# One weight ring and one set of PSUM banks through a hybrid gMLP and forgetting-attention block

## The chip, the cores and the metric

The kernel runs on one core of a Trainium2 chip. The metric is device time in microseconds (us) of one execution. In float32 the whole block is computed to almost full precision: every matmul operand is split into a high part (a cast to `float32r`) and a low part (what the cast lost), and each product is three matmuls, low by high, high by low, high by high.

## The reference

```python
h = rmsnorm(x, norm_mix_g)                       # x: 512 rows x 1024
z = h @ w_in                                     # u, v (gMLP), q, k, v (attention), f, two gates
uv = gelu(z[..., :2048]);  z_u, z_v = uv[..., :1024], uv[..., 1024:]
gates = sigmoid(z[..., o3:])                     # 2 x 1024 columns
a = z_u * (W_s @ layernorm(z_v) + b_s)           # per block of 128 rows and group of 128 columns
b = forgetting_attention(q, k, v, f_logit, b_f)  # 16 heads of 64
merged = gate_a * (a @ w_branch_a) + gate_b * (b @ w_branch_b)
x = x + merged @ w_out
h2 = rmsnorm(x); up = causal_depthwise_conv(h2 @ w_up)
x = x + (gelu(up[..., :2816]) * up[..., 2816:]) @ w_down
x = x + (p @ w_ple) * sigmoid(rmsnorm(x) @ w_ple_gate)
return rmsnorm(x)
```

## The kernel before

TensorE (PE) follows an order written out by hand almost everywhere (`tc.manual_schedule(engines={PE})`); ScalarE (ACT), VectorE (DVE), GpSimd (POOL) and the DMA queue of SyncE (SP) each get an order that a planner lays down before the run. At run time each of these queues is worked in that order: what waits holds up what stands behind it.

The stages, in the order of PE's work:

1. **Start.** Rows of `x` come in four blocks of 128. For each block `rms_x` squares and scales it, and `transpose_split` transposes it on PE in two groups of four and splits it into `hT`. A third copy of the transposed rows (`keep`, into the tile `zv`) serves the next stage but one. Between the blocks PE works on the first half of `p @ w_ple` (`pp`) and of the attention's v columns (`pv`). Then the 16 forget logits (`L550`), the second half of v, and gate chunk 0.
2. **Wino.** The u and v columns of gMLP (`wino_jobs`) are products by a 2x2 Strassen-Winograd scheme, seven block products P1, P7, P6, P2, P5, P4, P3 for `zv` and seven for `zu`, each 24 matmuls. Eight raw weight tiles are loaded per set; DVE combines them (`combine`: t3 makes the operand of P7 from tiles (1,1) and (0,1), then t2, t1, t4), `split_w` splits them. Then layernorm of `zv`, whose gains and offsets are broadcast loads into `gb`.
3. **Mix.** Eight `mix(g)` steps (masked block mixing, times u, transposed to DRAM `aT_d`), woven with gate chunks.
4. **Attention.** Eight pairs of heads. While pair `pr` is transposed and multiplied with v, the softmax of pair `pr+1` runs and the q and k projections of pair `pr+2` (`qk_pair`, two chunks of 24 matmuls) and gate chunks (24 matmuls each) fill PE in between (`weave`: items of the attention with `n` fill steps spread over them).
5. **Merge and the rest.** The attention output `o32` is split into `oT`, the last gate chunk runs, then `w_branch_b`, `w_branch_a`, `w_out`, the convolutional FFN and the final stage.

A *gate chunk* is one 128-column piece of the 16 gate projections: a weight load of 512 KB, its split, 24 matmuls, a copy out of PSUM (`place()` gives the SBUF tile) and a store to DRAM. Chunks have no hurry before the merge, so they serve as filler: before the change chunk 0 runs before the wino stage, 1 to 3 in the mix, 4 at the head of attention, one in each of pairs 0 to 5, two in pair 6, two in pair 7, and chunk 15 after attention.

Weights go through a *ring*: `load_w` takes a raw tile, a high and a low tile, issues the load on SP, and casts on ACT (L130) and subtracts on DVE or POOL (L131). There are two rings, one after the other: `ring0` with 8 raw tiles and 4 pairs of split tiles until the mix, and `ring` with 3 raw tiles and 5 pairs from attention on. Small tiles of 4 KB per partition called `mid`, three in all, serve for the forget gate's work (`fm`), gate chunks' copies, `gb`, and the mixing weights `wst`. The eight PSUM banks are shared out three times: four tags of two banks, then `c` 6 and `f` 2 for wino and mix, then `mm` 2, `sc` 2, `pt` 3, `av` 1 for attention, then four tags of two again.

Of the kernel before, what the change touches and what calls it, by code (L numbers as in the profile page):

```python
# [41 lines left out]
def hybrid_block(  # L42
# [24 lines left out]
    small = ctx.enter_context(tc.tile_pool(name="small", bufs=4, side="left"))  # L67
    state = {"n": 0, "bank": 0, "ring": None, "pool": {}, "psum": None}

# [14 lines left out]
    def bank(tag=None):  # L84
        pool, bufs = state["psum"]
        if tag is None:
            tag = f"b{state['bank'] % len(bufs)}"
            state["bank"] += 1
        return pool.tile([P, 512], F32, tag=tag, name=uid("bank"), bufs=bufs[tag])
# [24 lines left out]
    def open_ring(name, nbuf, raw=RAW_BUFS):  # L114
        es, pool = open_pool(name, "left")
        state["ring"] = (pool, nbuf, raw)
        return es


    def load_w(src, a, b, sub=None, later=None):  # L120


        pool, nbuf, nraw = state["ring"]
        raw = pool.tile([P, a, b], F32, tag="raw", name=uid("raw"), bufs=nraw)
        hi = pool.tile([P, a, b], F32R, tag="whi", name=uid("whi"), bufs=nbuf)
        lo = pool.tile([P, a, b], F32R, tag="wlo", name=uid("wlo"), bufs=nbuf)
        nc.sync.dma_start(raw, src)

        def split():
            A.copy(hi, raw)  # L130
            (sub or V).tensor_tensor(lo, raw, hi.bitcast(F32), ALU.subtract)  # L131
        if later is not None:
            later.append(split)
        else:
            split()
        return hi, lo
# [95 lines left out]
    def split_w(raw):  # L232
# [5 lines left out]
        return hi, lo  # L238

    def wino_jobs(wv, c0, act, sums, evac):  # L240


        pool, _, nraw = state["ring"]
        B, banks = {}, {}

        def load():
            for i, h in ((0, 0), (1, 1), (0, 1), (1, 0)):
                B[i, h] = []
                for j in range(2):
                    raw = pool.tile([P, 2, 512], F32, tag="raw", name=uid("raw"), bufs=nraw)  # L250
                    k, c = 4 * i + 2 * j, c0 + 512 * h
                    nc.sync.dma_start(raw, wv[:, k:k + 2, c:c + 512])
                    B[i, h].append(raw)
# [17 lines left out]
        def product(name, a, k0, col, acc, fresh):  # L271

            skip = not fresh

            def f(ws):
                if fresh:
                    banks[acc] = [bank("c") for _ in range(2)]
                for j in range(2):
                    for r in range(2):
                        out_ap, cs = banks[acc][r], ds(col + r * P, P)  # L280
                        for kk in range(2):
                            k = k0 + 2 * j + kk
                            wh, wl = ws[j][0][:, kk, :], ws[j][1][:, kk, :]
                            T.matmul(out_ap, a[1][:, k, cs], wh,  # L284
                                     start=(fresh and j == 0 and kk == 0), stop=False,
                                     skip_group_check=skip)
                            yield
                            T.matmul(out_ap, a[0][:, k, cs], wl, start=False, stop=False,  # L288
                                     skip_group_check=skip)
                            yield  # L290
                            T.matmul(out_ap, a[0][:, k, cs], wh, start=False,  # L291
                                     stop=(j == 1 and kk == 1), skip_group_check=skip)
# [88 lines left out]
    def transpose_split(src, dst, rb, n=NK, keep=None):  # L381

        done = []
        for k0 in range(0, n, 4):
# [7 lines left out]
            done.append((at, bk))  # L392
        if keep is not None:
            for at, bk in done:
                A.copy(keep[at], bk)

    def rms_x(src, g_bc, dst, rb):
# [49 lines left out]
    def zv_tile():  # L447
        return ph.tile([P, 4096], F32, tag="zv", name=uid("zv"))

    def mid(dt=F32):  # L450
        return ph.tile([P, D], dt, tag="mid", name=uid("mid"), bufs=3)

# [10 lines left out]
    with tc.manual_schedule(engines={ET.PE, ET.Activation, ET.DVE, ET.SP}):  # L463
# [36 lines left out]

        warm = mid()[:, 0:P]
        V.memset(warm, 0.0)
# [15 lines left out]
        steps(pp, 6)  # L518
        tx[0]()
        tx.append(rms_x(xt[1], gmix, hT, 1))  # L520
# [3 lines left out]
        steps(pv, 12)  # L524
        tx[1]()
        steps(pv, 12)
    with tc.manual_schedule(engines={mybir.EngineType.PE}):
        for rb in range(2, NB):
            tx.append(rms_x(xt[rb], gmix, hT, rb))
            steps(pv, 8)  # L530
            tx[rb]()
            steps(pv, 16)
        steps(pv, 24)


    fm = [mid(), mid(), mid(F32R)]
    bft = consts.tile([P, 1], F32, tag="bft", name="bft")
# [57 lines left out]

    psum.close()


    psum = open_psum("psumS", WINO_BANKS)
    zv = zv_tile().rearrange("p (b c) -> p b c", b=NB)  # L600
# [14 lines left out]

    def gate_steps(n, tag, place):

        w = load_w(w_in_v[:, :, gate_col(n):gate_col(n) + P], 8, P, sub=None)
        bk = bank(tag)
# [29 lines left out]
    with tc.manual_schedule(engines={ET.PE}):  # L649
        run(gate_steps(0, "f", lambda: mid()[:, 0:512]))  # L650
        units = wino_steps(wino_jobs(w_in_v, 1024, hT, sums, wino_rows(zv, gelu_zv))
                           + wino_jobs(w_in_v, 0, hT, sums, wino_rows(zu, gelu_zu)))
        steps(units, 168)
        gb = [mid(), mid()]
        nc.sync.dma_start(gb[0], rows_bc(ln_g[0], D))
        nc.sync.dma_start(gb[1], rows_bc(ln_b[0], D))

        wst = mid().rearrange("p (g s) -> p g s", g=8)
        nc.sync.dma_start(wst, w_s[0].rearrange("g t s -> t g s"))
# [10 lines left out]
        for rb in range(NB):  # L670
            A.activation(zv[:, rb, :], zv[:, rb, :], AF.Identity, bias=nm[:, rb:rb + 1])
            for h in range(2):
                A.activation(bank("f"), zv[:, rb, 512 * h:512 * h + 512], AF.Square,
                             accum_out=sq[:, NB * h + rb:NB * h + rb + 1])
# [9 lines left out]
        wsT = [quarter(f"S1{t}").rearrange("p (g t) -> p g t", g=8) for t in "hl"]  # L684
        bk = bank("f")
        T.transpose(bk[:, 0:P], bsr, ident)
        V.tensor_copy(bsT, bk[:, 0:NK])
        steps(units, 12)
        for g0 in (0, 4):
            bk = bank("f")  # L690
            for g in range(4):
# [5 lines left out]
        def mix(g):  # L697
# [3 lines left out]
            split_out((vh, vl), zv[:, :, c], (slice(None),) * 3)  # L701
            bk = bank("c")
            mm3(bk, wsT[0][:, g, :], wsT[1][:, g, :], vh, vl, True, True)
# [3 lines left out]
            yield  # L707
            bk = bank("c")
            for n in range(NB):
# [7 lines left out]
        run(units)  # L717

        w_qk0 = qk_weights(0)
        ms = [mix(g) for g in range(NK)]  # L720
# [3 lines left out]
        items += [ms[NK - 2], ms[NK - 1]]  # L724
        fill = chain(*(gate_steps(n, "f", lambda: mid()[:, 0:512]) for n in range(N_FIRST, N_FIRST + N_MIX)))
        weave(items, fill, 24 * N_MIX)
# [3 lines left out]
    ph_es.close()  # L730
    psum.close()
    ring.close()


    ring = open_ring("ring", 5)
    psum = open_psum("psumB", ATT_BANKS)
    att_es, att = open_pool("att", "right")
    o32 = k_view(slot(4, F32))

    for t in ("pth", "ptl"):  # L740
        att.tile([P, 1280], F32R, tag=t, name=uid(t), bufs=2)

# [107 lines left out]
    pts = [[[], []] for _ in range(NPAIR)]  # L850

    with tc.manual_schedule(engines={mybir.EngineType.PE}):
        run(qk_pair(0, w_qk0, qk[0]))
        cm[0], cm[1] = cum_pair(0), None
        sm = [softmax_head(qk[0], cm[0], a, probs[0][a]) for a in range(2)]
        fill = chain(qk_pair(1, qk_weights(1), qk[1]), gate_early(N_FIRST + N_MIX))
        for _ in range(12):
# [3 lines left out]
        for pr in range(NPAIR):  # L861
            fill = [gate_early(n) for n in range(GATES[pr], GATES[pr + 1])]
            n_fill = 24 * len(fill)
            if pr + 2 < NPAIR:
                fill.insert(0, qk_pair(pr + 2, qk_weights(pr + 2), qk[pr + 2]))
                n_fill += 48
# [16 lines left out]
    att_es.close()  # L883
    psum.close()
    psum = open_psum("psumC", FREE_BANKS)

# [13 lines left out]
    with tc.manual_schedule(engines={ET.PE}):  # L900
        for n in range(GATES[-1], N_GATES):
            run(gate_steps(n, None, lambda: scr.tile([P, S], F32, tag="gy", name=uid("gt"), bufs=2)))
    for k0 in (0, 4):
# [22 lines left out]

    def gated(wv, act, n0):

        c0 = P * (n0 % NK)
        sgs = []  # L930
        for i in range(2):
# [3 lines left out]
            sgs.append(sg)  # L935
        py = pieces_T(wv, c0)
        for i in range(2):
# [6 lines left out]
    for c0 in range(0, D, 256):  # L944
        for by, sg, c in gated(w_b_v, oT, c0 // P):
            V.tensor_tensor(sg, by, sg, ALU.mult)
# [254 lines left out]
```

## Time and profile before

| | before |
|---|---|
| median of 3 runs | 985.09 us (984.2 to 985.59) |
| the profiled execution | 985.49 us |
| its span in the profile | 983.7 us |
| PE busy | 943.7 us, 96% |
| DVE, ACT, POOL busy | 594.6, 466.5, 115.2 us |
| HBM traffic | 122 GB/s over the span |
| chain of work that ended last | PE 88%, DVE 6%, ACT 2%, DMA 2%, issue 1%, POOL 1% |

The span is what the profile shows from the first to the last instruction; 1.8 us of the execution lie around it. A time in a timeline row is the start in us from the span's start; the second number is the duration; a bracket at the end says how long the engine had stood idle before the row and what released it. Matmul rows carry modelled ends, so the distance between the starts of two neighbours is the true pace of PE.

### The profile page before, as it was taken

What the parts mean: (1) busy time and instruction counts of PE and PEld (TensorE: products, weight loads), DVE (VectorE), ACT (ScalarE), POOL (GpSimd) and SP (SyncE); (2) the same over time, 40 slices, a digit from 0 to 9 for tenths busy, and PEclk for the clock granted to TensorE, in tenths of its full rate; (3) what the DMA queues carried; (4) which work ended last, traced back from release to release, by engine and by line L of the source; (5) the groups of instructions that cost most, each with busy time, mean ns of one, the idle gap of its engine ahead of it and who ended that gap; (6) DMA issues with size and microseconds to landing.
All of it is one profiled execution on the core that took longest, in us unless ns stands there. A gap on an engine that the chain in (4) does not pass through costs nothing.

```text
span 983.7 us, 11724 instructions
## 1 busy us (share of the span) xinstructions
PE 943.7 (96%) x4375; PEld 780.0 (79%) x4375; DVE 594.6 (60%) x1017; ACT 466.5 (47%) x779; POOL 115.2 (12%) x94
## 2 busy tenths in 40 slices
PE   6999996979999999799999999999999999999996
PEld 5788885867888888688888788888888888888885
DVE  4787888538777788623344756555346663355664
ACT  6554684346666666522334544444124442144453
POOL 2100000022222200000121400000000000000225
PEclk9999998989999999999999999999999999999998
DMA  9352340664333332296864233323223333223202
GB/s 331 128 152 83 121 108 1 220 169 133 106 101 97 97 97 86 65 338 230 265 188 158 65 118 118 106 86 107 90 67 101 110 105 106 86 86 110 75 31 85
DMA packets 102148, 121.21 MB, mean 123 GB/s; under 512 B 5252, under 2 KB 70972, under 8 KB 102092
## 3 DMA queue, kind: packets, MB, share of 16 engines
q1 hardware_dynamic: 101948, 120.21, 38.7%
q8 instruction: 34, 0.56, 0.2%
q10 hardware_dynamic: 144, 0.26, 0.1%
q14 instruction: 22, 0.18, 0.1%
HBM read 106.79 MB, written 13.66 MB: 122 GB/s over the span
## 4 chain that ended last, share of the span: by engine, by line
PE 88%; DVE 6%; ACT 2%; DMA 2%; issue 1%; POOL 1%; SPq 0%; POOLq 0%; DVEq 0%
PE bank L153 17%; PE bank L157 16%; PE bank L155 16%; PE bank L140 5%; PE bank L141 5%; PE bank L139 5%; PE bank L213 3%; PE bank L217 3%; PE bank L215 3%; PE bank L288 2%; PE bank L284 2%; PE bank L291 2%; PE bank L832 2%; PE bank L823 2%; DMA raw<-in_w_in_dram 2%
## 5 line engine op out<-in xcount | busy, mean ns | idle before, releaser
L153 PE MATMUL bank<-slot,wlo 128*128 128x512 f32 (+1 forms) x744 | 297.4, 401 | 11.3 <-DVE wlo L131 6.2
L155 PE MATMUL bank<-slot,whi 128*128 128x512 f32 (+1 forms) x744 | 290.5, 391 | 0.0
L157 PE MATMUL bank<-slot,whi 128*128 128x512 f32 (+1 forms) x744 | 290.4, 391 | 0.0
L130 ACT CAST whi<-raw 128x1024 fp32r<-128x1024 f32 x140 | 145.9, 1047 | 130.7 <-PE bank L141 76.2
L131 DVE TENSOR_TENSOR wlo<-raw,whi 128x1024 fp32r<-128x1024 f32 x116 | 143.1, 1237 | 106.1 <-ACT whi L130 105.5
L153 PEld LDWEIGHTS bank<-slot,wlo 128*128 128x128 f32 x744 | 141.2, 190 | 35.6 <-issue 6.6
L157 PEld LDWEIGHTS bank<-slot,whi 128*128 128x128 f32 x744 | 140.7, 189 | 29.0
L155 PEld LDWEIGHTS bank<-slot,whi 128*128 128x128 f32 x744 | 141.2, 190 | 22.7
L131 POOL TENSOR_TENSOR wlo<-raw,whi 128x1024 fp32r<-128x1024 f32 x24 | 59.4, 2481 | 486.6 <-ACT whi L130 480.9
L139 PE MATMUL bank<-whi,slot 128*128 128x512 f32 (+1 forms) x232 | 88.6, 382 | 0.0
L141 PE MATMUL bank<-whi,slot 128*128 128x512 f32 (+1 forms) x232 | 88.6, 382 | 0.0
L140 PE MATMUL bank<-wlo,slot 128*128 128x512 f32 (+1 forms) x232 | 88.6, 382 | 0.0
L213 PE MATMUL bank<-whi,slot 128*128 128x512 f32 x152 | 60.6, 399 | 2.1 <-DVE slot L352 2.1
L217 PE MATMUL bank<-whi,slot 128*128 128x512 f32 x152 | 60.1, 395 | 0.0
L215 PE MATMUL bank<-wlo,slot 128*128 128x512 f32 x152 | 59.6, 393 | 0.0
L140 PEld LDWEIGHTS bank<-wlo,slot 128*128 128x128 f32 x232 | 43.6, 188 | 8.5
L141 PEld LDWEIGHTS bank<-whi,slot 128*128 128x128 f32 x232 | 43.6, 188 | 8.5
L139 PEld LDWEIGHTS bank<-whi,slot 128*128 128x128 f32 x232 | 43.6, 188 | 8.4
L1041 DVE SCALAR_TENSOR_TENSOR ul<-bank,cvT,ul 128x511 f32<-128x511 f32 x22 | 16.5, 750 | 51.7 <-ACT ul L1040 51.7
L237 DVE TENSOR_TENSOR wlo<-raw,whi 128x1024 fp32r<-128x1024 f32 x28 | 33.9, 1221 | 13.1 <-ACT whi L236 13.0
L805 ACT ACTIVATE t<-t,mn 128x512 f32<-128x512 f32 (+1 forms) x64 | 36.0, 562 | 12.4 <-DVE mn L802 8.9
L236 ACT CAST whi<-raw 128x1024 fp32r<-128x1024 f32 x28 | 29.4, 1051 | 22.8 <-PE bank L291 17.0
(265 smaller groups left out, 1320.5 us busy)
## 6 DMA issues: line engine op xcount, KB each, us to landing
raw<-in_w_in_dram SPq DMA_DIRECT2D x56, 512.0 KB, 4.0
raw<-in_w_up_dram SPq DMA_DIRECT2D x44, 512.0 KB, 3.6
raw<-in_w_down_dram SPq DMA_DIRECT2D x22, 512.0 KB, 3.4
cum<-cum_d SPq DMA_DIRECT2D x8, 512.0 KB, 4.0
raw<-in_w_branch_b_dram SPq DMA_DIRECT2D x8, 512.0 KB, 4.1
slot<-aT_d SPq DMA_DIRECT2D x4, 1024.0 KB, 13.3
sg<-gate_d SPq DMA_DIRECT2D x16, 256.0 KB, 3.8
raw<-in_w_branch_a_dram SPq DMA_DIRECT2D x8, 512.0 KB, 8.7
```

The source lines that it names most:

```text
L130: A.copy(hi, raw)
L131: (sub or V).tensor_tensor(lo, raw, hi.bitcast(F32), ALU.subtract)
L139: T.matmul(out_ap, alo, bhi, start=start, stop=False)
L140: T.matmul(out_ap, ahi, blo, start=False, stop=False)
L141: T.matmul(out_ap, ahi, bhi, start=False, stop=stop)
L153: T.matmul(out_ap, wl, ah, start=(n == 0 and k == 0), stop=False)
L155: T.matmul(out_ap, wh, al, start=False, stop=False)
L157: T.matmul(out_ap, wh, ah, start=False, stop=end)
L213: T.matmul(bk, alo[:, k, r], wh, start=(k == 0), stop=False)
L215: T.matmul(bk, ahi[:, k, r], wl, start=False, stop=False)
L217: T.matmul(bk, ahi[:, k, r], wh, start=False, stop=(k == nk - 1))
L805: A.activation(t, t, AF.Exp, scale=-1.0, bias=m, accum_out=rs[:, i:i + 1])
```

## The change

- One ring (5 split pairs, 3 raw tiles) and one set of banks (`mm` 2, `sc` 2, `pt` 3, `av` 1) live through the whole kernel. Where no tag is named, banks are taken in the order of `BANK_TURN`.
- Until attention begins, a pool `more` of 5 tiles adds to the raw tiles: of every 8 loads, counted through, numbers 1, 2 and 8 go to the ring's own raw tiles and numbers 3 to 7 to `more`. The pool `mid` is gone: gate chunks' copies, `gb` and `wst` take tiles of `more`, and the forget gate's work and the warm-up tile take `S4h`, `S4l` and `S2l`, which the start and the wino sums use too.
- The `keep` copies of a block of rows are issued after the next block's transposes.
- Gate chunk 1 runs alone between wino and mix (`N_COVER`); the mix is woven with chunks 2 to 4, attention begins with 5, and each of pairs 0 to 5 has the chunk one higher; pair 6 has one chunk (12) where it had two.
- During the last chunk of the mix the q and k weights of pairs 0 and 1 are queued; during the last chunk of attention the weights of chunk 15 and of the first 256 columns of `w_branch_b`.

```diff
-GATES = [5, 6, 7, 8, 9, 10, 11, 13, 15]
+GATES = [6, 7, 8, 9, 10, 11, 12, 13, 15]
-FREE_BANKS = {"b0": 2, "b1": 2, "b2": 2, "b3": 2}
-WINO_BANKS = {"c": 6, "f": 2}
-ATT_BANKS = {"mm": 2, "sc": 2, "pt": 3, "av": 1}
+N_COVER = 1
+X_BUFS = 5
+BANKS = {"mm": 2, "sc": 2, "pt": 3, "av": 1}
+BANK_TURN = ["mm", "sc", "pt", "mm", "sc", "pt", "pt", "av"]
...
+    def raw_tile(a, b):
+        pool, _, nraw = state["ring"]
+        if state["more"]:
+            state["raw"] += 1
+            if state["raw"] % (nraw + X_BUFS) >= nraw:
+                return more_tile().rearrange("p (a b) -> p a b", a=a)
+        return pool.tile([P, a, b], F32, tag="raw", name=uid("raw"), bufs=nraw)
+
+    def more_tile():
+        return state["more"].tile([P, D], F32, tag="more", name=uid("more"), bufs=X_BUFS)
...
-        if keep is not None:
+        def copy():
             for at, bk in done:
                 A.copy(keep[at], bk)
+        return copy
...
-    ring = open_ring("ring0", 4, 8)
-    psum = open_psum("psumA", FREE_BANKS)
+    ring = open_ring("ring", 5)
+    more_es, state["more"] = open_pool("more", "left")
+    psum = open_psum("psum", BANKS)
...
-    fm = [mid(), mid(), mid(F32R)]
+    fm = [quarter("S4h", F32), quarter("S4l", F32), quarter("S2l")]
...
-        run(gate_steps(0, "f", lambda: mid()[:, 0:512]))
+        run(gate_steps(0, "mm", lambda: more_tile()[:, 0:512]))
...
         run(units)
-        w_qk0 = qk_weights(0)
+        for n in range(N_FIRST, N_FIRST + N_COVER):
+            run(gate_steps(n, "mm", lambda: more_tile()[:, 0:512]))
...
+        def preload(g):
+            next(g)
+            yield
+            w_qk.extend(qk_weights(pr) for pr in range(2))
+            yield from g
...
+    def preload_merge(g):
+        next(g)
+        yield
+        w_merge.append(gate_weights(N_GATES - 1))
+        w_merge.append(pieces_T(w_b_v, 0))
+        yield from g
```

More of the change, by code (lines that the diff above doesn't have):

```diff
@@ L67, in hybrid_block @@
     small = ctx.enter_context(tc.tile_pool(name="small", bufs=4, side="left"))
-    state = {"n": 0, "bank": 0, "ring": None, "pool": {}, "psum": None}
+    state = {"n": 0, "bank": 0, "ring": None, "more": None, "raw": 0, "pool": {}, "psum": None}
     def uid(s):
@@ L86, in bank @@
         if tag is None:
-            tag = f"b{state['bank'] % len(bufs)}"
+            tag = BANK_TURN[state["bank"] % len(BANK_TURN)]
             state["bank"] += 1
@@ L249, in load @@
                 for j in range(2):
-                    raw = pool.tile([P, 2, 512], F32, tag="raw", name=uid("raw"), bufs=nraw)
+                    raw = raw_tile(2, 512)
                     k, c = 4 * i + 2 * j, c0 + 512 * h
@@ L276, in f @@
                 if fresh:
-                    banks[acc] = [bank("c") for _ in range(2)]
+                    banks[acc] = [bank(t) for t in WINO_BANKS[acc]]
                 for j in range(2):
@@ L497, in hybrid_block @@
         pv = proj_N_steps(w_in_v[:, :, 4096:5120], 0, NK, hT, 0, evac_v, subs=w_v0)
-        warm = mid()[:, 0:P]
+        warm = quarter("S4l", F32)[:, 0:P]
         V.memset(warm, 0.0)
@@ L524, in hybrid_block @@
         steps(pv, 12)
-        tx[1]()
+        copy1 = tx[1]()
+        copy0()
         steps(pv, 12)
@@ L653, in hybrid_block @@
         steps(units, 168)
-        gb = [mid(), mid()]
+        gb = [more_tile(), more_tile()]
         nc.sync.dma_start(gb[0], rows_bc(ln_g[0], D))
         nc.sync.dma_start(gb[1], rows_bc(ln_b[0], D))
-        wst = mid().rearrange("p (g s) -> p g s", g=8)
+        wst = more_tile().rearrange("p (g s) -> p g s", g=8)
         nc.sync.dma_start(wst, w_s[0].rearrange("g t s -> t g s"))
@@ L684, in hybrid_block @@
         wsT = [quarter(f"S1{t}").rearrange("p (g t) -> p g t", g=8) for t in "hl"]
-        bk = bank("f")
+        bk = bank("mm")
         T.transpose(bk[:, 0:P], bsr, ident)
@@ L689, in hybrid_block @@
         for g0 in (0, 4):
-            bk = bank("f")
+            bk = bank("mm")
             for g in range(4):
@@ L701, in mix @@
             split_out((vh, vl), zv[:, :, c], (slice(None),) * 3)
-            bk = bank("c")
+            bk = bank("sc")
             mm3(bk, wsT[0][:, g, :], wsT[1][:, g, :], vh, vl, True, True)
@@ L707, in mix @@
             yield
-            bk = bank("c")
+            bk = bank("pt")
             for n in range(NB):
@@ L724, in hybrid_block @@
         items += [ms[NK - 2], ms[NK - 1]]
-        fill = chain(*(gate_steps(n, "f", lambda: mid()[:, 0:512]) for n in range(N_FIRST, N_FIRST + N_MIX)))
+        w_qk = []
+        def preload(g):
[3 more added lines that the diff above has]
+            yield from g
+        fill = [gate_steps(n, "mm", lambda: more_tile()[:, 0:512]) for n in range(GATES[0] - 1 - N_MIX, GATES[0] - 1)]
+        fill = chain(*fill[:-1], preload(fill[-1]))
         weave(items, fill, 24 * N_MIX)
@@ L730, in hybrid_block @@
     ph_es.close()
[L731 to L736, printed above, removed]
+    more_es.close()
+    state["more"] = None
     att_es, att = open_pool("att", "right")
     o32 = k_view(slot(4, F32))
-    for t in ("pth", "ptl"):
-        att.tile([P, 1280], F32R, tag=t, name=uid(t), bufs=2)
     kzs = []
@@ L900, in hybrid_block @@
     with tc.manual_schedule(engines={ET.PE}):
-        for n in range(GATES[-1], N_GATES):
-            run(gate_steps(n, None, lambda: scr.tile([P, S], F32, tag="gy", name=uid("gt"), bufs=2)))
+        run(gate_steps(N_GATES - 1, None,
+                       lambda: scr.tile([P, S], F32, tag="gy", name=uid("gt"), bufs=2), w_merge[0]))
     for k0 in (0, 4):
```

38 lines of the change are left out of this document (20 added, 18 removed).

## The prediction

> **What bounds the kernel now.** I read the page's busy times first, then the table of waits of PE, then the timeline around each wait.
>
> ```profile
> PE 943.7 (96%) x4375; PEld 780.0 (79%) x4375; DVE 594.6 (60%) x1017; ACT 466.5 (47%) x779; POOL 115.2 (12%) x94
> ```
>
> PE is the bound: what it computes doesn't change (the same chunks and products, in another order), so only its idle time and its slow stretches can be won, 40 us at most of idle. The table of waits names them (who waited, for whom; us in total, times, longest):
>
> ```profile
> PE bank L153 <- DVE wlo L131: 6.2, 1, 6.2
> PE bank L153 <- ACT gt L622: 5.1, 1, 5.1
> PE bank L388 <- DVE S4l L404: 4.1, 2, 2.1
> PE bank L139 <- DVE S1l L352: 3.2, 1, 3.2
> PE bank L140 <- DVE S2h L352: 2.7, 1, 2.7
> PE bank L692 <- DVE bsT L687: 1.7, 1, 1.7
> ```
>
> The first five, 21.3 us, lie at the four places that the change touches: the first is the q weights of pair 1, the second gate chunk 15 behind attention, the third the start, the fourth and fifth the head of the mix. From 60 us to the mix PE waits for nothing but the bsT row, so the wino stage has no wait to lose and some to gain. PE's pace, from the first and last of chunk 0's 24 matmuls:
>
> ```profile
> 73.89 0.39 PE L153 MATMUL bank<-slot,wlo 128*128 128x512 f32 x1
> 79.10 0.39 PE L157 MATMUL bank<-slot,whi 128*128 128x512 f32 x1
> ```
>
> 23 steps in 5.21 us: 0.227 us a matmul, 5.45 a chunk or a wino product.
>
> **The change part by part.**
>
> *Weights of pair 1 (gain 8.1 us).* PE's timeline:
>
> ```profile
> 202.96 0.39 PE L157 MATMUL bank<-slot,whi 128*128 128x512 f32 x1
> 209.58 0.77 PE L153 MATMUL bank<-slot,wlo 128*128 128x512 f32 x1 [6.23 <-DVE wlo L131]
> ...
> 213.09 0.39 PE L157 MATMUL bank<-slot,whi 128*128 128x512 f32 x1
> ```
>
> The next start was due at 203.19 and came at 209.58: 6.39 us. The 8 matmuls from there to 213.09 took 3.51 us instead of 1.82: 1.69 more at half pace. Together 8.1. The queues show why:
>
> ```profile
> 194.06 4.21 SPq L127 DMA_DIRECT2D raw<-in_w_in_dram  x3
> ...
> 206.64 0.58 ACT L772 CAST st<-bank 64x512 fp32r<-64x512 f32 x1 [0.76 <-DVE st L771]
> 207.13 2.94 ACT L130 CAST whi<-raw 128x1024 fp32r<-128x1024 f32 x3
> ...
> 208.20 3.50 DVE L131 TENSOR_TENSOR wlo<-raw,whi 128x1024 fp32r<-128x1024 f32 x3 [1.60 <-ACT whi L130]
> ```
>
> The weights' loads were issued from 194 on, but their casts stand in ACT's queue behind the copies of pair 0's k, when the old ring's tiles are free. In the one ring the two pair-1 weights take the split tiles of chunks 2 and 3, whose matmuls end inside the mix; their loads are ring tiles that u's weights left long before. The casts and subtractions of both pairs (4 of each, 0.98 and 1.17 us) then fall into the mix beside PE's 16 items and three chunks; without that cover each costs its length. SP gets the same loads, earlier, ahead of the stores of `aT_d`, for which nobody waits before the merge. Next late would be the first scores, 12 matmuls after 203.19, at 205.9: k's last copy, of head 1, ends at 207.2 (the 206.64 row), head 0's before it, so up to 1.3 may come back. Bounds: 5 to 8.1; I take 8.1.
>
> *Chunk 15 after attention (gain 7.1 us).*
>
> ```profile
> 411.97 0.39 PE L157 MATMUL bank<-slot,whi 128*128 128x512 f32 x1
> 417.43 0.80 PE L153 MATMUL bank<-slot,wlo 128*128 128x512 f32 x1 [5.07 <-ACT gt L622]
> ...
> 421.35 0.39 PE L153 MATMUL bank<-slot,wlo 128*128 128x512 f32 x1
> ```
> ```profile
> 411.73 4.30 DVE L352 TENSOR_TENSOR slot<-slot,slot 128x512 fp32r<-128x512 f32 x7 [3.48 <-PE bank L832]
> 416.06 0.70 DVE L841 TENSOR_TENSOR slot<-bank,ot 64x512 f32<-64x512 f32 x1
> ```
> ```profile
> 416.79 0.59 ACT L622 COPY gt<-bank 128x512 f32<-128x512 f32 x1 [1.52 <-DVE slot L841]
> ```
>
> Chunk 15 got the bank of chunk 14, whose copy (L622) waits for the only `ot` tile, which waits for L841 behind seven splits of `oT`. In the one set chunk 15 takes an `mm` bank in turn, that is chunk 13's, emptied long before. It starts at 412.20, 5.23 us earlier, without the slow stretch (9 matmuls in 3.92 us instead of 2.05: 1.87). Together 7.1. Next is `w_branch_b`: its eighth row of `oT` waits for L841 (done at 416.8), a cast and a subtraction of 0.61 (4.30 for seven), so 418; PE wants it 21 matmuls into the first piece, at 422. Its weights and chunk 15's, three loads, casts and subtractions, move up into pair 7 under two chunks of PE's work. If a subtraction still fell behind the seven splits, it would cost up to 3. Bounds: 4 to 7.1; I take 7.1.
>
> *Head of the mix (gain 7.1 us).*
>
> ```profile
> 158.29 0.40 PE L291 MATMUL bank<-whi,S4h 128*128 128x512 f32 x1
> 161.87 0.76 PE L139 MATMUL bank<-S2h,S1l 128*128 128x512 f32 x1 [3.18 <-DVE S1l L352]
> 165.31 0.80 PE L140 MATMUL bank<-S2h,S1h 128*128 128x512 f32 x1 [2.67 <-DVE S2h L352]
> ...
> 168.78 0.39 PE L141 MATMUL bank<-S2l,S1h 128*128 128x512 f32 x1
> ```
> ```profile
> 164.56 0.69 DVE L352 TENSOR_TENSOR S2h<-zv,S2h 128x512 fp32r<-128x512 f32 x1
> ```
>
> The two late starts cost 3.35 and 3.21 us and the 8 matmuls to 168.78 1.65 more: 8.2. Now chunk 1 (24 matmuls, 5.45 us) stands before: PE comes to the mix at 163.97, DVE still delivers at 165.25, so 1.1 us stay. Gain 7.1; the chunk is not extra work, it is one less later. The loads of `gb` and `wst` now wait on SP until t4 and the splits of u's weights free their tiles:
>
> ```profile
> 134.54 1.22 DVE L257 TENSOR_TENSOR raw<-raw,raw 128x1024 f32<-128x1024 f32 x1
> ...
> 147.04 4.86 DVE L679 SCALAR_TENSOR_TENSOR zv<-zv,qy,mid 128x1024 f32<-128x1024 f32 x4
> ```
>
> The last step of t4 ends at 135.8; `gb` is asked for at 147.04, so a load has 11 us. Behind it on SP stand only chunk weights that wait for the same tiles. Bounds: 3.4 (three more subtractions of 1.17 ahead of the mix's) to 8.2.
>
> *Start (gain 3.5 us).*
>
> ```profile
> 17.42 1.18 ACT L395 COPY zv<-bank 128x512 f32<-128x512 f32 x2 [1.31 <-DVE slot L352]
> 18.50 1.06 ACT L401 ACTIVATE S4l<-slot 128x1024 f32<-128x1024 f32 x1
> 21.66 3.52 DVE L404 SCALAR_TENSOR_TENSOR S4l<-slot,ry,S1l 128x512 f32<-128x512 f32 x2
> ...
> 25.98 0.78 PE L213 MATMUL bank<-whi,slot 128*128 128x512 f32 x1
> ...
> 28.69 0.85 PE L213 MATMUL bank<-whi,slot 128*128 128x512 f32 x2
> ```
>
> The square of block 1 (18.50) stands behind the two `keep` copies and the wait before them: 2.4 us (1.31, and the copies to 18.50). From it hang the scaling (to 25.2) and PE's wait for it (4.1 in the table). With the copies behind the next transposes the chain comes 2.4 us earlier, and of the slow stretch (7 steps in 2.71 us and one more, 1.3 us too long) most goes. 3.5. The copies themselves then hold two banks longer; eight come in turn, and the transposes of the block after next are the first to ask for one. Bounds: 0 (the forget weights now load into `S4l` only after block 3's transposes, and the logits on PE follow soon) to 5.
>
> *A wait that the change adds: P7 of zv (loss 6.3 us).* Counting loads: 1 to 5 at the start, 6 to 9 for v, 10 chunk 0, 11 to 18 the eight wino tiles. `more` gets 3 to 7, then chunk 0's copy, then 11 to 14, then 15: with five tiles, load 15 gets the one that chunk 0's copy holds until its store has landed. Load 15 is half of tile (0,1), which t3 needs for P7. That a tile is held from its turn in the program on, not from its first use, the queue of SP shows today: the load of `wst` (L659), which reads an input and needs only a `mid`, waits for chunk 0's store.
>
> ```profile
> SPq L252 <- DVE wlo L131: 31.4, 5, 20.3
> ...
> SPq L659 <- DMA gate_d<-mid: 1.6, 1, 1.6
> ```
> ```profile
> 82.16 0.38 SPq L659 DMA_DIRECT2D mid<-in_gmlp_w_s_dram  x1
> ```
> ```profile
> DMA to landing us min/median/max: 3.7/3.9/5.6
> ```
>
> Load 15 can go at 82.16 at best, lands 3.9 us later (the last row, of the wino loads), t3 takes 1.22, the cast 0.98, the subtraction 1.17: 89.4. P1 ends at 79.33 + 5.45 = 84.8, so P7 is 4.6 us late (3.4 to the cast, then 1.2), and a slow stretch of 1.7 follows, as at the mix. Loads 16 to 18 take ring tiles and don't wait for it; behind load 15 on SP stands nothing that PE needs before zu. Bounds: 0 (if the load isn't held) to 8.0 (5.6 us to land).
>
> The Trainium skill (TensorE: Matmul & The Clock Gate, What's actually happening) says that the clock halves only after a whole idle window of about 3.4 us, and that the windows run free of the program. By it a gap of 3.4 us mostly spans no whole window; the sum below would be 1.7 lower, 966.9. The mix's row, 3.18 and 2.67 us apart by one matmul, was followed by the slow pace, so the sum goes by the row.
>
> *Pair 6 with one chunk less (loss 2.6 us).* The columns are the stretch, its length, busy us of PE, PE's loads, DVE, ACT and POOL, clock, DMA:
>
> ```profile
> 375.00:394.50 19.50, 18.68 (x101) 15.53 (x100) 16.14 (x50) 11.84 (x29) 1.82 (x1) 1.00 0.26 82
> ```
> ```profile
> 380.66 0.33 PE L823 MATMUL bank<-ident,t 128*128 128x128 f32 x1 [0.81 <-DVE ptl L352]
> ```
>
> A chunk less takes 5.45 us from PE (13.2 left) and 1.2 from DVE (14.9 left): DVE becomes the bound of this pair. The stretch would be 14.05 if PE still set it; 14.9 if DVE does without a gap (loss 0.9), 18.3 with DVE's gaps of now (loss 4.2). Middle: 2.6. Bounds 0 to 4.2.
>
> Bank names, the removed dummy tiles and the other pairs: nothing, eight banks still come in turn. The sum: 8.1 + 7.1 + 7.1 + 3.5 - 6.3 - 2.6 = 16.9 us won, from the profiled execution's 985.49 (span 983.7 and 1.8 around it; 0.4 above the median): **968.6**, given as 969.
>
> **The rivals.**
>
> - *No wait at P7* (chunk 0's copy gets its tile late, or the load is hidden): 985.49 - 23.2 = 962.3. For it: PE waits for no wino operand today. Against it: the L659 row.
> - *The gains shrink*: DVE late at the mix (3.7 less), pair 6 at 4.2 (1.6 more), nothing at the start (3.5 less): 968.6 + 8.8 = 977.4. For it: both late starts of the mix wait for DVE. Against: the two subtractions of pair 0's weights, which the code put ahead of the mix, now come behind its first items.
> - *The early loads don't help*, since casts and subtractions still stand behind later work in ACT's and DVE's queues: 968.6 + 8.1 + 7.1 = 983.8, no change that can be told. For it: the cast at 207.13. Against: with one ring the tiles are free before the mix ends, and chunk 15's bank is another one whatever the queues do. The Trainium skill (Perfetto Trace Analysis, Per-engine timelines) states that these engines take instructions strictly in order; the trace agrees: ACT stood idle 0.76 us before the copy that is ahead of that cast.
> - *Slower: wino tiles run short.* Eight raw tiles now also hold chunk copies, `gb` and `wst`. Each further product of the 14 that waits like P7 costs 6.3; three more give 968.6 + 18.9 = 987.5, slower from there on. For it: SP waited 31.4 us for raw tiles (the L252 row) though all eight were theirs. Against it: of the tiles taken ahead of the last wino load, chunk 0's copy is the only one that is held idle; `gb`, `wst` and the later chunks come behind u's eight.
>
> **How the numbers follow.** Forecast 0.53, its own range 964 to 975; no wait at P7 0.17; shrunken gains 0.18; no help 0.06; slower 0.06. A run of this kernel tells 0.2% (2 us) from no change. Faster: the first three and a little of the fourth, 0.89; same 0.05; slower 0.06. The range: 960 is 2 us under the second case, 981 takes in the third with 3 us to spare; outside lie the last two cases and the second's tail.
>
> **What the profile after would show.** The rows of wlo L131, of gt L622 and of the mix gone from PE's waits; matmuls at full pace behind them; a new wait of 4 to 5 us at L284 near 80 to 85 us, with SP's load waiting for the store of chunk 0; waits on ptl or mn in pair 6; the second transposes of the start near 22. The prediction is wrong if one sees: that new wait absent, any wait in zu, forget logits waiting for their weights, or pair 6 as long as before.

## The result: slower by 0.8%, and the profile after

| | before | after |
|---|---|---|
| median | 984.68 us (984.2 to 985.59, 4 runs) | 992.8 us (991.71 to 994.18, 4 runs) |
| ratio to before | | 1.0082, 95% interval 1.0065 to 1.01 |
| the profiled execution, its span | 985.49, 983.7 us | 993.0, 991.2 us |

The forecast was 969 us, faster. First the busy line of the page after, and four rows of PE's table of waits (us in total, times, longest):

```profile
PE 945.1 (95%) x4375; PEld 779.5 (79%) x4375; DVE 597.6 (60%) x1017; ACT 465.5 (47%) x779; POOL 113.7 (11%) x94
```
```profile
PE bank L167 <- DVE wlo L145: 17.2, 3, 7.4
PE bank L153 <- DVE slot L367: 3.5, 1, 3.5
PE bank L299 <- ACT whi L250: 2.9, 2, 1.6
PE bank L303 <- DVE wlo L251: 1.6, 2, 0.8
```

Lines have moved: L167 after is L153 before (a weight chunk's first matmul), L144 and L145 are the cast and the subtraction of `load_w`, L299 to L306 the wino products, L153 the products with rows of activations, here `w_out`. PE computes what it computed before. The waits for `gt` and at the head of the mix are gone, as forecast; but the wait for weights (wlo) is 17.2 us in three pieces where it was 6.2 in one, and L299, L303 and L153 are new. Where they lie, in PE's timeline after:

```profile
75.09 0.49 PE L299 MATMUL bank<-whi,slot 128*128 128x512 f32 x1 [1.62 <-ACT whi L250]
76.35 0.50 PE L303 MATMUL bank<-wlo,slot 128*128 128x512 f32 x1 [0.77 <-DVE wlo L251]
...
84.76 0.50 PE L299 MATMUL bank<-whi,S3l 128*128 128x512 f32 x1 [1.28 <-ACT whi L250]
86.08 0.50 PE L303 MATMUL bank<-wlo,S3h 128*128 128x512 f32 x1 [0.82 <-DVE wlo L251]
...
157.06 0.66 PE L711 MATMUL bank<-ident,more 128*128 128x128 f32 x4 [0.92 <-DVE bsT L706]
...
169.36 0.52 PE L167 MATMUL bank<-slot,wlo 128*128 128x512 f32 x1 [3.01 <-DVE wlo L145]
...
186.41 0.79 PE L167 MATMUL bank<-slot,wlo 128*128 128x512 f32 x1 [6.77 <-DVE wlo L145]
...
204.02 0.80 PE L167 MATMUL bank<-slot,wlo 128*128 128x512 f32 x1 [7.39 <-DVE wlo L145]
...
534.88 0.80 PE L153 MATMUL bank<-whi,slot 128*128 128x512 f32 x1 [3.47 <-DVE slot L367]
```

The three long ones are the first matmuls of gate chunks 2, 3 and 4, woven into the mix, where PE waited for no chunk's weights before. Since both kernels run the same 4375 matmuls, the start of the n-th one in two traces tells where time was won or lost. The table gives the change of that difference from before, per stretch (us; minus is won; stretches bounded by the matmul numbers in the head; what the stretches leave out is under 0.5 in all). Each row comes from one profiled execution:

| | start, 0-95 | forget to chunk 0, 95-314 | first wino products, 314-350 | mix to pair 1, 640-1000 | pairs and chunk 15, 1000-1890 | w_out, 2330-2375 | all |
|---|---|---|---|---|---|---|---|
| forecast | -3.5 | 0 | +6.3 | -15.2 | -4.5 | 0 | -16.9 |
| after | -6.0 | 0.0 | +7.2 | +6.8 | -5.9 | +5.3 | +7.5 |
| E1 own copies | -6.3 | +5.4 | 0.0 | -14.6 | -3.1 | +4.9 | -13.7 |
| E2 PSUM reopened | -5.8 | 0.0 | +8.3 | +7.4 | -5.7 | +1.8 | +6.5 |
| E3 no cover | -6.3 | 0.0 | +8.6 | +4.5 | -5.7 | +4.3 | +5.8 |
| E4 q, k as before | -5.7 | 0.0 | +8.6 | +1.2 | -4.4 | +2.1 | +2.0 |
| E5 six of `more` | -4.6 | 0.0 | +7.9 | -3.4 | -5.8 | +4.8 | -1.2 |
| E6 own copies, four | -6.2 | 0.0 | 0.0 | -3.6 | -4.4 | +5.6 | -8.6 |
| E7 own forget tile | -5.8 | +0.2 | 0.0 | -15.1 | -3.1 | +6.0 | -17.8 |
| E8 four gates | -5.7 | +0.2 | 0.0 | -15.1 | -4.8 | 0.0 | -25.4 |
| E9 before, late copies | -5.8 | 0.0 | 0.0 | 0.0 | +0.4 | 0.0 | -5.3 |
| E10 before, other bank | 0.0 | 0.0 | 0.0 | -0.2 | -7.1 | +0.7 | -6.5 |
| E11 E8 without cover | -6.0 | +0.2 | 0.0 | -9.8 | -5.9 | 0.0 | -21.6 |
| E12 E8, q, k as before | -6.4 | +0.2 | 0.0 | -14.3 | -4.8 | 0.0 | -25.4 |

The forecast misses by 24.4 us: 22.0 in the mix, 5.3 at `w_out`, 0.9 at wino; the start and the pairs were 2.5 and 1.4 better. Why the chunks' weights are late, SP's queue after shows (start and time from the first to the last of a group):

```profile
143.40 9.32 SPq L141 DMA_DIRECT2D more<-in_w_in_dram  x2
166.37 0.34 SPq L642 DMA_DIRECT2D gate_d<-more  x1
175.02 1.61 SPq L733 DMA_DIRECT2D aT_d<-S4h  x2
178.22 1.04 SPq L733 DMA_DIRECT2D aT_d<-S4l  x2
179.37 0.39 SPq L141 DMA_DIRECT2D more<-in_w_in_dram  x1
...
196.95 0.43 SPq L141 DMA_DIRECT2D more<-in_w_in_dram  x1
...
198.65 0.47 SPq L141 DMA_DIRECT2D more<-in_w_in_dram  x1
```
```profile
SPq L642 <- ACT more L641: 13.6, 1, 13.6
SPq L733 <- ACT S4h L366: 8.2, 1, 8.2
```

The second fence is the first two rows of SP's waits from 160 to 180 us. Chunk 3's load at 179.37 stands behind the store of chunk 1's copy, for which SP waited 13.6 us, and behind four stores of `aT_d`, for the first of which it waited 8.2. The tile was not what it lacked: counted through in the program's order, this load takes the tile of `wst`, whose last transposes are the PE row at 157.06. Chunk 4's load (196.95) takes the tile of chunk 1's copy, stored at 166.37, and the first of q and k (198.65) that of chunk 2's weights, cast at 166.91; both go out 30 us or more after that, behind further stores. ACT after, the copy of chunk 1 and the casts of chunks 2 and 3:

```profile
165.76 0.59 ACT L641 COPY more<-bank 128x512 f32<-128x512 f32 x1 [3.43 <-PE bank L171]
...
166.91 1.04 ACT L144 CAST whi<-more 128x1024 fp32r<-128x1024 f32 x1
...
184.06 1.04 ACT L144 CAST whi<-more 128x1024 fp32r<-128x1024 f32 x1 [3.73 <-DMA more<-in_w_in_dram]
```

Two things are seen. Chunk 2's load went out by 152.7, but its cast (166.91) stands behind chunk 1's copy, for which ACT idled 3.43 us with nothing else it was allowed to do: this is the wait of 3.01. The Trainium skill (Perfetto Trace Analysis, Per-engine timelines) says ACT and DVE take their instructions strictly in order; this row agrees. Chunk 3's cast waited for the load itself (3.73): this is the wait of 6.77. Chunk 4's, at 201.67, did the same (4.41), and PE waited 7.39.

### The profile page after: what moved, and what is told of

Same layout as the page of the kernel before. It is cut to its first block, busy times and chain, and to the rows that moved or that the text cites. A ratio compares the mean times of both kernels' runs of the same rounds, so it can differ in the third digit from the quotient of the medians.

```text
span 991.2 us, 11717 instructions
## 1 busy us (share of the span) xinstructions
PE 945.1 (95%) x4375; PEld 779.5 (79%) x4375; DVE 597.6 (60%) x1017; ACT 465.5 (47%) x779; POOL 113.7 (11%) x94
## 4 chain that ended last, share of the span: by engine, by line
PE 75%; DMA 10%; DVE 8%; ACT 3%; issue 2%; POOL 1%; SPq 0%; POOLq 0%; ACTq 0%; DVEq 0%
PE bank L167 14%; PE bank L169 13%; PE bank L171 13%; PE bank L153 5%; PE bank L154 5%; PE bank L155 5%; DMA sg<-gate_d 4%; PE bank L227 3%; PE bank L231 3%; PE bank L229 3%; DMA gyb_d<-sg 2%; PE bank L303 2%; PE bank L306 2%; PE bank L299 2%; PE bank L856 2%
## 5 line engine op out<-in xcount | busy, mean ns | idle before, releaser
L167 PE MATMUL bank<-slot,wlo 128*128 128x512 f32 (+1 forms) x744 | 296.8, 400 | 18.1 <-DVE wlo L145 17.2
L144 ACT CAST whi<-raw 128x1024 fp32r<-128x1024 f32 x130 | 135.5, 1046 | 112.7 <-PE bank L155 67.9
L145 DVE TENSOR_TENSOR wlo<-raw,whi 128x1024 fp32r<-128x1024 f32 x108 | 136.3, 1266 | 85.0 <-ACT whi L144 84.7
L167 PEld LDWEIGHTS bank<-slot,wlo 128*128 128x128 f32 x744 | 140.8, 189 | 44.0 <-DVE wlo L145 15.0
L145 POOL TENSOR_TENSOR wlo<-raw,whi 128x1024 fp32r<-128x1024 f32 x22 | 53.9, 2453 | 543.5 <-ACT whi L144 543.5
L153 PE MATMUL bank<-whi,slot 128*128 128x512 f32 (+1 forms) x232 | 89.4, 386 | 3.5 <-DVE slot L367 3.5
L153 PEld LDWEIGHTS bank<-whi,slot 128*128 128x128 f32 x232 | 44.0, 190 | 12.5 <-DVE slot L367 3.9
L366 ACT CAST pth<-bank 128x512 fp32r<-128x512 f32 (+1 forms) x64 | 26.3, 428 | 24.9 <-PE bank L847 24.7
L1012 DVE TENSOR_TENSOR slot<-bank,slot 128x512 f32<-128x512 f32 x32 | 21.7, 687 | 23.3 <-PE bank L155 13.8
```

What stands on the lines that cost most here:

```text
L153: T.matmul(out_ap, alo, bhi, start=start, stop=False)
L167: T.matmul(out_ap, wl, ah, start=(n == 0 and k == 0), stop=False)
```

## The experiments

Medians are of 4 to 10 runs; the kernel before had 984.7 to 985.6 beside them. Brackets are 95% intervals of the ratio to before. The times of E2 and E3 overlap those of the changed kernel, and E7's those of E1; there the table of stretches tells what the edit did.

**E1: copies in their own tiles.**

```diff
+    def gate_copy():
+        return ph.tile([P, S], F32, tag="gc", name=uid("gc"), bufs=2)
...
-        run(gate_steps(0, "mm", lambda: more_tile()[:, 0:512]))
+        run(gate_steps(0, "mm", gate_copy))      # and so for chunks 1 to 4
```

> Edit: the changed kernel, but the copies of gate chunks 0 to 4 get two tiles of their own instead of tiles of `more`. Theory A (copies and loads share one row of tiles, and get them in the program's order, so the loads come to stand in SP's queue behind the copies' stores and the stores of aT_d): the loads of the chunks' weights at 179.37, 196.95 and 198.65 us go before the mix, the three waits in the mix (17.2 us, and about 5 of slow pace behind them) go, and so does most of the 7.2 us lost at the first wino products: 992.8 - 17 - 5 - 7 = 964. Rival B (the casts stand in ACT's queue behind the chunks' copies, whichever tile holds these): the 3.0 us wait and the loss at wino stay, the two waits for late loads (6.8 and 7.4) go: 977. Rival C (the early q and k weights take the split tiles): 993, no change.

970.65 us (965.43 to 971.75), ratio 0.9836 [0.9806, 0.9865]: 22 us faster than the changed kernel by 4 KB more per partition, in two half tiles. Its SP queue:

```profile
33.27 0.37 SPq L560 DMA_DIRECT2D S4l<-in_w_in_dram  x1
...
135.73 3.73 SPq L141 DMA_DIRECT2D raw<-in_w_in_dram  x3
141.61 12.41 SPq L141 DMA_DIRECT2D more<-in_w_in_dram  x5
```

All five loads in question (chunks 1 to 4, first q) go by 154.0, ahead of every store of the mix, and wlo is gone from PE's waits. Mix to pair 1 comes to -14.6, where -15.2 was forecast; the loss at wino is 0. Theory A holds, B and C fall. But 5.4 us go elsewhere: PE waited for the forget weights. Their load, now behind four wino loads, went out at 33.27, which is no later than in the changed kernel (33.55). What moved is the subtraction of their low part, which stands further back in DVE's queue. PE's wait in E1, then the subtraction in E1 and in the changed kernel:

```profile
PE bank L568 <- DVE S2l L562: 3.5, 1, 3.5
```
```profile
45.55 0.28 DVE L562 TENSOR_TENSOR S2l<-S4l,S2l 128x128 fp32r<-128x128 f32 x1
```
```profile
38.24 0.28 DVE L562 TENSOR_TENSOR S2l<-S4l,S2l 128x128 fp32r<-128x128 f32 x1
```

Why the planner put it there is not shown.

**E2: PSUM reopened behind attention.**

```diff
     att_es.close()
+    psum.close()
+    psum = open_psum("psumC", BANKS)
```

> Edit: the changed kernel, but the PSUM set is closed behind attention and the same eight banks are opened again. Theory D (without that border a load of w_branch_b moves in SP's queue ahead of the loads of aT_d, of the conv weights and of the first gates, and SP stands 15.1 us for its tile; the row of gates then ends late at w_out): SP asks for the first gates some 15 us earlier, PE's wait of 3.5 us at 534.88 goes with the slow pace behind it: 992.8 - 5.3 = 987.5. If chunk 15 again waits for a bank, 5 to 7 come back: 993 to 995. Rival E (the loss at w_out comes from the weights of chunk 15 and of w_branch_b that are asked for a chunk early): 993, and the wait at w_out stays.

991.37 us (989.79 to 992.05), 1.0061 [1.0046, 1.0076]; at `w_out` +1.8 instead of +5.3, the wait is 1.5 us instead of 3.5. So the missing border cost 3.5 of the 5.3, and D holds in part; the time gained less than that, 1.4, since among others 1.1 more was lost at the first wino products, which the edit doesn't touch. What the border does is seen best on PE: the last transposes of the last head, after and in E2:

```profile
415.71 0.38 PE L847 MATMUL bank<-ident,t 128*128 128x128 f32 x2
...
421.17 0.27 PE L847 MATMUL bank<-ident,t 128*128 128x128 f32 x1
```
```profile
418.09 0.38 PE L847 MATMUL bank<-ident,t 128*128 128x128 f32 x2
...
419.10 0.33 PE L847 MATMUL bank<-ident,t 128*128 128x128 f32 x1
```

5.46 us between them after, 1.01 in E2: with one set of banks the planner moves 20 matmuls of chunk 15 between these two transposes, so attention ends that much later for everyone but PE. SP is the second part. Its queue after, then the same gates in E2 and before:

```profile
416.38 15.91 SPq L141 DMA_DIRECT2D raw<-in_w_branch_b_dram  x2
...
448.61 1.05 SPq L967 DMA_DIRECT2D sg<-gate_d  x2
```
```profile
440.23 2.59 SPq L969 DMA_DIRECT2D sg<-gate_d  x2
```
```profile
428.41 2.93 SPq L933 DMA_DIRECT2D sg<-gate_d  x2
```

The first gates are asked for 20.2 us later than before, while PE is only 2.2 behind there. From them a chain of load, sigmoid, product and store or split runs through two tiles to the end of the merge; its end is the new wait. How much of the 3.5 belongs to the matmuls and how much to SP was not separated.

**E3: without the cover chunk.** `N_COVER = 0`, `GATES = [5, 6, ...]` as before.

> Edit: the changed kernel without the chunk between projections and mix; its chunk goes back behind the last scores. Theory A: the copies still stand among the loads, so two or three waits for chunk weights stay, and the head of the mix waits again for its splits, 3 to 8 us: 996 to 1000. Rival F (the chunk at the head causes the waits, since its copy and its store stand ahead of the next chunk's load and cast): the waits of 3.0 and 6.8 us and about 4 of slow pace go, 7 come back at the head, 2 are won in pair 6: 984 to 987.

991.16 us (988.87 to 993.25), 1.0061 [1.0042, 1.008]. Both long waits for chunk weights stay:

```profile
181.07 0.79 PE L167 MATMUL bank<-slot,wlo 128*128 128x512 f32 x1 [6.58 <-DVE wlo L145]
...
198.97 0.80 PE L167 MATMUL bank<-slot,wlo 128*128 128x512 f32 x1 [7.35 <-DVE wlo L145]
```

Only the 3.01 goes with the cover chunk (and comes back as 2.7 at the mix's head). Rival F falls; theory A's number was too high by 5.

**E4: q and k weights asked for as before.**

```diff
-        w_qk = []
+        w_qk = [qk_weights(0)]
...
-            w_qk.extend(qk_weights(pr) for pr in range(2))
...
-        fill = chain(qk_pair(1, w_qk[1], qk[1]), ...)
+        fill = chain(qk_pair(1, qk_weights(1), qk[1]), ...)
```

> Edit: the changed kernel, but the weights of q and k are asked for where they were before: pair 0 ahead of the mix, pair 1 behind it. Theory A: one chunk's load less stands behind stores, so one wait of 7 less in the mix, and pair 1's weights wait again, 6 to 8: 990 to 994. Rival C (the early q and k weights cause the waits of the mix): the waits of 6.8 and 7.4 us go with 4 of slow pace, 8 come back at pair 1: 983.

989.26 us (987.48 to 989.74), 1.0037 [1.0024, 1.005]: 3.5 better than the changed kernel, a little below A's range. Two waits of 13.8 us together stay, so rival C falls again. Both lie in the mix (175.26 and 192.19): PE does not wait for pair 1's weights, though the code asks for them as late as before, and the 6 to 8 us that A expected there did not come back.

**E5: six tiles of `more`, copies among the loads.** `X_BUFS = 6`.

> Edit: the changed kernel with six tiles of `more` instead of five; the copies of the chunks stay among the loads. This has as much memory as the first experiment. Theory A (what hurts is that copies take their turn among the loads): chunk 4's load and the first q and k weights still stand behind stores, so one or two waits of about 7 us stay in the mix, and so does the loss at the first wino products: 980 to 993. Rival G (it was only one tile too few): as the first experiment, 970.

985.01 us (979.38 to 987.27), 0.9986 [0.9968, 1.0005]. With the memory of E1 it is 14 us slower than E1. PE and SP in it:

```profile
196.09 0.80 PE L167 MATMUL bank<-slot,wlo 128*128 128x512 f32 x1 [7.46 <-DVE wlo L145]
```
```profile
188.96 0.43 SPq L141 DMA_DIRECT2D more<-in_w_in_dram  x1
```

The sixth tile shifts the count, so that chunks 1 to 3 load into the ring's own tiles and are in time; chunk 4, whose tile is one of `more`, still loads at 188.96, and 7.46 us are lost as in the changed kernel. Within A's range, and 15 above G's number.

**E6: own copies, `more` of four.** E1 with `X_BUFS = 4`, no more memory than the changed kernel.

> Edit: the copies of chunks 0 to 4 get two half tiles of their own, and `more` has four tiles instead of five; this is no more memory than the changed kernel has. Theory A: no wait for chunk weights in the mix, none at the first wino products: 968 to 973. Rival G (one tile too few): as the changed kernel, 990 to 995.

975.25 us (973.54 to 976.86), 0.9897 [0.9883, 0.9912]. No wait for a chunk and none at wino; 10 us faster than E5 with less memory. That settles rival G for these waits. It is 2 over A's range: `gb` is asked for at 132.56, in E1 at 126.90, the layernorm starts later, and PE waits for the row of `bsT` that stands behind it in DVE's queue:

```profile
PE bank L714 <- DVE bsT L709: 7.8, 1, 7.8
```

**E7: the forget weights in a copy's tile.**

```diff
-    wf_raw = fm[1][:, 512:].rearrange("p (k c) -> p k c", k=8)
+    wf_raw = ph.tile([P, S], F32, tag="gc", name=uid("wf"), bufs=2).rearrange(...)
```

> Edit: the first experiment, and the forget weights load into one of the copies' tiles instead of the second half of S4l. Theory H (the forget weights' load waits for S4l and stands in SP's queue behind loads that wait for tiles; this cost 5.1 us between the 95th and the 200th matmul): the load goes out near 15 us, PE's wait of 3.5 us for the forget weights goes with the slow pace behind it: 970.6 - 5.1 = 965.5. Rival: DVE prepares them late for another reason: 970.

966.63 us (963.57 to 969.54), 0.981 [0.9785, 0.9835]. The load moves from 33.27 to 11.22, the subtraction from 45.55 to 24.41, and PE's wait is gone: +5.4 becomes +0.2; 1.2 of it come back at `w_out`, whose wait grows from 3.0 to 4.3. Theory H's time holds, its cause only in part: a load at 33 us alone cost nothing in the changed kernel. SP's queue:

```profile
11.22 0.38 SPq L560 DMA_DIRECT2D wf<-in_w_in_dram  x1
```

**E8: four gate tiles.** E7 with `bufs=4` instead of 2 for the tag `sg`.

> Edit: the seventh experiment, and four tiles for the gates (sg) in the merge instead of two. Theory I (a gate's tile is held from its load to the split of its product, so the row of gates cannot run ahead of PE and ends late at w_out): gates load two ahead, PE's wait of 3.0 us and the slow pace at w_out go: 965.5 - 4.9 = 960.6. Rival: SP's queue or the transfers set the row of gates: 965, and the wait stays.

960.41 us (960.24 to 960.8), 0.9748 [0.9733, 0.9762]: faster than both kernels, by 2.5% and 3.3%. Four gates load in one go, and the wait at `w_out` is gone from PE's table, whose longest row now is the second here:

```profile
421.08 6.79 SPq L970 DMA_DIRECT2D sg<-gate_d  x4
```
```profile
PE bank L850 <- DVE ptl L367: 4.3, 4, 1.7
```

Theory I holds: it was the count of tiles, not the transfers.

**E9: before, with the late `keep` copies alone** (the `copy()` part of the diff shown above).

> Edit: the kernel before, and of the change only the delayed copies of the untransposed x blocks (each block's copies behind the next block's transposes). The changed kernel gained 6.0 us between its start and the 95th matmul, all from this if theory K holds (the square of block 1 no longer stands behind two copies in ACT's queue, and the slow pace behind the wait goes whole): 985.4 - 6.0 = 979.4. By the prediction's own sum the part is worth 3.5: 981.9. If the 6.0 came from the forget weights' other tiles and their loads: 985.

980.31 us (980.23 to 980.61), 0.9951 [0.9934, 0.9968]; the stretch is worth 5.8. Theory K holds.

**E10: before, with another bank for chunk 15.**

```diff
-    state["bank"] = 0
+    state["bank"] = 1
     with tc.manual_schedule(engines={ET.PE}):
         for n in range(GATES[-1], N_GATES):
```

> Edit: the kernel before, and chunk 15 behind attention starts the turn of the banks at the second tag instead of the first, so it gets another bank than chunk 14's. Everything else stays. The prediction's term: the wait of 5.07 us and the slow pace behind it go, 7.1 us: 978.3. Theory L (the row of gates, which starts from attention's end, has some 5 us to spare at w_out; what PE gains before it beyond that comes back as a wait there): 1.5 to 2 us come back: 980. If the loss of 5.3 at w_out in the changed kernel comes from this gain alone, 5.3 come back: 983.6.

979.14 us (978.52 to 980.2), 0.994 [0.9925, 0.9954]. One digit wins 7.1 at its place; 0.7 come back at `w_out`, less than L's 1.5 to 2, so the row of gates had some 6.4 us to spare. Of the changed kernel's 5.3 there, this gain explains 0.7.

**E11: E8 without the cover chunk.** The constants of E3.

> Edit: the eighth experiment without the chunk between projections and mix (it goes back behind the last scores). Here no load waits behind a copy, so the chunk shows its own worth. The prediction's terms: 7.1 lost at the head of the mix, 2.6 won in pair 6: 960.4 + 4.5 = 964.9. Rival M (the splits of the mix are ready in time by now, since DVE has less to catch up): 958 to 960.

963.72 us (963.03 to 964.96), 0.9783 [0.9769, 0.9798]: 3.3 slower than E8. The head of the mix waits again, 1.4 us at 154.57 and then

```profile
158.08 0.79 PE L154 MATMUL bank<-S2h,S1h 128*128 128x512 f32 x1 [3.01 <-DVE S2h L367]
```

By the table the chunk is worth 5.3 in the mix and costs 1.1 in the pairs. Rival M falls.

**E12: E8 with q and k asked for as before.** The edit of E4.

> Edit: the eighth experiment with the weights of q and k asked for where they were before: pair 0 ahead of the mix, pair 1 behind it. The prediction's term for asking early is 8.1 us: 968.5. Rival N (the one ring is enough: its tiles are free, so the planner puts the loads early in SP's queue wherever the code asks for them): 960 to 962.

960.29 us (959.6 to 960.42), 0.9746 [0.9731, 0.976]: no difference from E8. Three loads into the ring's own tiles, pair 1's two among them, go out at the same place in both kernels, here in E12 and then in E8:

```profile
130.16 3.73 SPq L141 DMA_DIRECT2D raw<-in_w_in_dram  x3
```
```profile
130.63 3.46 SPq L141 DMA_DIRECT2D raw<-in_w_in_dram  x3
```

Rival N holds: with one ring the planner issues them when a tile is free, wherever the code asks.

## Why the prediction was wrong, step by step

- **Start: right, too small.** 3.5 forecast, 5.8 alone on the kernel before (E9). The prediction gave the chain 2.4 us and most of the slow stretch; in E9 the wait for the scaling went from 4.1 to 1.7, and the slow stretch behind it went whole.
- **Pair 1's weights: right, with one part idle.** 8.1 forecast; in E11, where no cover chunk shifts the count, the 60 matmuls around this wait (820 to 880) win 8.1. Of the two things that the change does there, the one ring and the early request, the ring alone does it (E12, and E4 before it).
- **Chunk 15: right.** 7.1 forecast, 7.1 measured by the bank alone (E10).
- **Head of the mix and pair 6: right in sign.** 7.1 and -2.6 forecast, 5.3 and -1.1 in E8 against E11.
- **Wino: right size in part by luck, half the mechanism.** 6.3 forecast, 7.2 measured. As forecast, a load stands behind the store of chunk 0's copy, and a slow stretch follows. But three loads stand there, not one, and the first casts stand behind the copy itself on ACT, so that P1 waits too: the 4.6 us of idle that were forecast at P7 are 2.1 there (1.28 and 0.82) and 2.4 at P1 (1.62 and 0.77). The rows are ACT's, then SP's, after:

```profile
73.51 0.58 ACT L641 COPY more<-bank 128x512 f32<-128x512 f32 x1 [4.85 <-PE bank L171]
73.99 2.00 ACT L250 CAST whi<-more 128x1024 fp32r<-128x1024 f32 x2
```
```profile
74.12 0.34 SPq L642 DMA_DIRECT2D gate_d<-more  x1
74.51 2.26 SPq L267 DMA_DIRECT2D more<-in_w_in_dram  x3
```

- **The step that failed** is the sentence on the mix's SP queue: "Behind it on SP stand only chunk weights that wait for the same tiles." The same cause that was priced at P7, a load that takes its turn behind a copy in one row of tiles, was not carried on to the mix: there the loads of chunks 3 and 4 come behind the copies of chunks 1 to 3 and so behind the stores of `aT_d`, while chunk 2's load is in time and its cast stands behind chunk 1's copy on ACT. E1 against after puts 21.4 us on it in this stretch. The prediction came near it in the slower rival, at a chance of 0.06, but in the wrong place. That of the tiles "taken ahead of the last wino load, chunk 0's copy is the only one that is held idle" is true. It priced three more late wino products at 18.9; what came late were three chunks, behind that load.
- **A term at nothing that wasn't:** "Bank names, the removed dummy tiles and the other pairs: nothing, eight banks still come in turn." The border that went with the PSUM sets held chunk 15 and a load of `w_branch_b` behind attention's end; without it 5.3 us were lost at `w_out`, 3.5 of them by E2. Chunk 15's gain explains 0.7 (E10); the other 1.1 stay open.
- **Forget logits** were named as a sign of error and did not wait in the changed kernel; the 5.4 us appeared in E1, where their load went out as early as before but their subtraction stood further back in DVE's queue.

## What to carry to other kernels

Tiles that are loaded ahead and tiles that hold a result until its store should not share one row of buffers: the turn of the tiles decides the order in the DMA queue, and one store that waits for its data holds every load behind it. When a pool or a PSUM set is merged with its neighbour, ask what its border kept in order, and write down the DMA queue's new order before pricing the gain. A gain of a few us ahead of a long chain off the critical path (here the row of gates) is worth only what that chain has to spare, until the chain gets more buffers.

## What the runs showed of the hardware that was not expected

Waits of the same size were followed by half pace at once, later, or not at all. (A row of 0.39 or 0.40 us belongs to a step of 0.23 us from start to start, a row of 0.63 to a step of 0.43.) At the first wino product, P1, the changed kernel and E4 have the same two waits, of 1.62 and of 0.77 or 0.76 us. E4 turns to half pace right behind the second; the changed kernel runs on at full pace for about 1 us and turns then, at 77.73. At P7 the changed kernel stays at full pace behind its waits of 1.28 and 0.82 us; E4, behind 1.41 and 0.81, turns to half pace again. The rows of the changed kernel, then of E4:

```profile
77.73 0.63 PE L299 MATMUL bank<-whi,slot 128*128 128x512 f32 x1
...
86.42 0.40 PE L306 MATMUL bank<-whi,S3h 128*128 128x512 f32 x1
```
```profile
76.72 0.79 PE L303 MATMUL bank<-wlo,slot 128*128 128x512 f32 x1 [0.76 <-DVE wlo L251]
...
86.76 0.63 PE L306 MATMUL bank<-whi,S3h 128*128 128x512 f32 x1
```

With one slow stretch the wino stretch costs 7.2, with two 8.6. Behind the waits of 3.01, 6.77, 7.39 and 3.47 us in the changed kernel full pace came back after 3.7, 3.9, 3.2 and 3.5 us, whatever the wait's length. The Trainium skill (TensorE: Matmul & The Clock Gate, What's actually happening) says that the clock is judged by windows of about 3.4 us that run free of the program; the chance in when half pace comes, and the length of the slow stretch, agree with that. It also says that half pace follows a whole idle window; that does not agree: at P1 1.62 and 0.77 us of idle with a matmul between were enough in both kernels.
